# Recurrent mixer of a three-block network: both heads of a pair in one step, products of the two heads interleaved

## Chip, cores and metric

One core of a Trainium2 chip runs the whole program. The metric is the time of one execution on the device in microseconds, and the number that counts is the median of several executions. Engines are named as in the profile: TensorE (PE; its weight loads PEld), VectorE (DVE), ScalarE (ACT), GpSimd (POOL), SyncE (SP).

## What is computed

Three blocks follow each other on one sequence of 512 tokens with 1024 channels. The change lies in the mixer of the first block, which computes two things from one projection: a recurrence over 8 heads of 64 channels (RWKV-7), and attention over a window of 128 tokens with 8 query heads. The reference, cut to that:

```python
p = h @ w_in                       # 512 x 1024 times 1024 x (1792 + 768)
# recurrent heads: state is 64 x 64 per head, w_t decay, kk_t and b_t from k and a
def step(state, inp):
    r_t, w_t, k_t, v_t, kk_t, b_t = inp
    sa = einsum('bhvk,bhk->bhv', state, -kk_t)
    state = (state * w_t[:, :, None, :] + sa[..., None] * b_t[:, :, None, :]
             + v_t[..., None] * k_t[:, :, None, :])
    return state, einsum('bhvk,bhk->bhv', state, r_t)
_, o = lax.scan(step, s0, ...)     # then a norm over each head, a bonus term, a gate
# attention: scores of a block of 128 queries with its own and the previous 128 keys
scores = einsum('bnqhgd,bnkhd->bnhgqk', qb, kb) * (HEAD_DIM ** -0.5)
probs = softmax(concatenate([masked scores, sink]))[..., :-1]
out = einsum('bnhgqk,bnkhd->bnqhgd', probs, vb)
x = x + concatenate([o_rwkv, o_attn]) @ w_out
```

## The kernel before

The kernel keeps channels on the 128 partitions and the 512 tokens along the free side. A **dense** product is a tile of 128 channels in and 128 out on 512 tokens; for precision it is done three times, with weights and activations split into a high and a low part (L390, L391, L392, on the two banks ps_d). A projection of 128 output channels is 24 of them. In the trace each dense product is one record, and each product of plain fp32 operands is two records.

The mixer of the first block (class Mixer1, function mixer_1) cuts the recurrence into 8 chunks of 64 tokens, so that it becomes products of 64x64 blocks. A **pair** i (0 to 3) is two heads, h = 0 and 1, whose 64 channels lie on the lower and the upper half of the partitions. Eight chunks are numbered c, or (j, e) with c = 2j + e. Five generators are stepped in turn by rounds, in the order of the letters of a string, here 'DZADHPHA':

- D, project: the 20 projections in the order of a list, three dense products a step, and at the end the output projection (mixed).
- P, per_token and pre: what each token of a pair needs, then its turned copies (L841 turns v, L854 and L863 turn k and b).
- H, heads and head: the chunk-local work of a pair. heads steps the two heads of a pair in turn.
- Z, all_states, states and finish: what links the chunks.
- A, attention and attend: four steps c of two query heads, four blocks j of 128 queries each.

The scheduler turns the steps into one instruction stream for each engine; each engine takes its stream in order. What one generator waits for is thus covered by what the others have put behind it in TensorE's stream.

The function head, for one head: two sets of four products of 64 rows and 128 columns (L918, tile pa, half e each), read by VectorE into X, kk and rb (L921 to L924); eight products pk (L928), read into ak and a4 (L930, L931); eight products pv (L938), copied by ScalarE into R; then a triangular inverse: two steps of px (L952) with X = 1 - px (L953), and for each of four levels l the products pw (L966, read into W, L969) and px (L973, taken off X), with VectorE's turning of X into T between. Each is a chain: product, VectorE, product. Eight products write both halves of a tile: the one for chunk (j, e) lies on the column half e, and its rows are on half e too, except for pk and pv. Last come four products on the whole array, pg (L988), whose results ScalarE puts into gk and gv (L997). Tiles are [128, 4, 64] and have two buffers, one for each head.

The function states, for a pair: three sets of sixteen products (L1015; 128 rows, 64 columns; eight chunks of head 0 and then eight of head 1) with a reader each; the chain of six steps through the chunks (L1032, L1033); two sets of sixteen for the output (L1042 and L1049, on the bank ps_z). finish: the gate product (L1063), its readers L1066 and L1067, the product for the variance (L1069), the norm and the result in bv. The last pair's result is split in two (k and r, L404 and L405) and read by the last products of the stage (L1191 to L1193, in the function last).

attend: scores of two heads (L1121: 64 rows, 128 columns, up to 256 streamed), each with its own bank of ps_p and its own step, softmax, turning of the weights on TensorE (L1145), and the output (L1152; 128 rows, 64 columns, head 0 on the column half 0, head 1 on the half 1).

The eight banks: ps_d 2, ps_m 3 (all of head, the sets of states, finish), ps_p 2, ps_z 1.

## Time and profile before

| what | value |
|---|---|
| median of the runs | 2809.36 us (2806.97, 2809.36, 2810.24) |
| the profiled execution | 2807.89 us; its span, from first to last instruction, 2806.0 us |
| TensorE busy | 2762.4 us, 98% of the span |
| VectorE, ScalarE, GpSimd busy | 60%, 41%, 3% |
| the stage from L841 at 412.73 to the end of L1049 at 722.69 | 309.96 us |

All times of the trace are from the start of that span. The span is 1.9 us shorter than the time of its execution, and this execution is 1.5 us below the median. A row of the timeline gives the start, the time until the last of its records ends, the engine, the line, the operation with out<-in, for a product the size of the part of the array that it uses (rows * columns) and the streamed operand, and the number of records. Products are pipelined: rows overlap, and the distance between two starts says what a product costs, not its length.

### The profile page before, as it was taken

What the parts mean: (1) busy time and instruction counts of PE and PEld (TensorE: products, weight loads), DVE (VectorE), ACT (ScalarE), POOL (GpSimd) and SP (SyncE); (2) the same over time, 40 slices, a digit from 0 to 9 for tenths busy, and PEclk for the clock granted to TensorE, in tenths of its full rate; (3) what the DMA queues carried; (4) which work ended last, traced back from release to release, by engine and by line L of the source; (5) the groups of instructions that cost most, each with busy time, mean ns of one, the idle gap of its engine ahead of it and who ended that gap; (6) DMA issues with size and microseconds to landing.
All of it is one profiled execution on the core that took longest, in us unless ns stands there. A gap on an engine that the chain in (4) does not pass through costs nothing. (4 is left out here: it accounts for less than half of the span.)

```text
span 2806.0 us, 36273 instructions
## 1 busy us (share of the span) xinstructions
PE 2762.4 (98%) x14502; PEld 2245.7 (80%) x14502; DVE 1682.7 (60%) x2795; ACT 1161.1 (41%) x1779; POOL 79.8 (3%) x167
## 2 busy tenths in 40 slices
PE   8999999999999999999999999999999999999998
PEld 7888877777788888777888888888887878888887
DVE  5443466777643436687344894646845985556456
ACT  4222354454332224575333433444457544343333
POOL 0000000000000000000000011110000000000000
PEclk9999999999999999999999999999999999999999
DMA  4333231101233333322343354443224443322232
GB/s 139 98 98 98 87 127 44 31 31 56 67 98 98 98 97 125 121 76 81 96 132 98 106 165 140 139 133 109 86 71 144 144 150 106 114 74 83 68 105 76
DMA packets 83866, 281.19 MB, mean 100 GB/s; under 512 B 10096, under 2 KB 10608, under 8 KB 82928
## 3 DMA queue, kind: packets, MB, share of 16 engines
q1 hardware_dynamic: 76464, 255.28, 28.3%
q0 software_dynamic: 5888, 18.09, 1.8%
q10 hardware_dynamic: 1344, 5.49, 0.5%
q8 instruction: 114, 1.87, 0.3%
q14 instruction: 56, 0.46, 0.1%
HBM read 254.44 MB, written 23.07 MB: 99 GB/s over the span
## 5 line engine op out<-in xcount | busy, mean ns | idle before, releaser
L366 ACT CAST whi<-raw 128x1024 fp32r<-128x1024 f32 (+4 forms) x454 | 450.6, 993 | 1204.3 <-PE ps_d L391 817.1
L390 PE MATMUL ps_d<-xhi,whi 128*128 128x512 f32 x1896 | 753.9, 398 | 12.7 <-ACT whi L366 8.1
L392 PE MATMUL ps_d<-xhi,wlo 128*128 128x512 f32 x1896 | 742.3, 392 | 3.4 <-DVE wlo L367 3.4
L391 PE MATMUL ps_d<-xlo,whi 128*128 128x512 f32 x1896 | 742.6, 392 | 0.2 <-DVE xlo L458 0.2
L367 DVE TENSOR_TENSOR wlo<-raw,whi 128x1024 fp32r<-128x1024 f32 (+4 forms) x454 | 521.4, 1149 | 156.3 <-ACT whi L366 155.0
L390 PEld LDWEIGHTS ps_d<-xhi,whi 128*128 128x128 f32 x1896 | 356.9, 188 | 93.1 <-ACT whi L366 8.6
L392 PEld LDWEIGHTS ps_d<-xhi,wlo 128*128 128x128 f32 x1896 | 357.0, 188 | 80.0 <-DVE wlo L367 4.9
L391 PEld LDWEIGHTS ps_d<-xlo,whi 128*128 128x128 f32 x1896 | 357.3, 188 | 75.5 <-issue 4.0
L390 PE MATMUL ps_d<-hh,whi 128*128 128x512 f32 x608 | 237.2, 391 | 0.4 <-ACT hh L404 0.4
L391 PE MATMUL ps_d<-hl,whi 128*128 128x512 f32 x608 | 237.0, 390 | 0.2 <-DVE hl L405 0.2
L392 PE MATMUL ps_d<-hh,wlo 128*128 128x512 f32 x608 | 236.7, 389 | 0.3 <-DVE wlo L367 0.3
L390 PEld LDWEIGHTS ps_d<-hh,whi 128*128 128x128 f32 x608 | 114.1, 188 | 25.1 <-ACT hh L404 0.9
L391 PEld LDWEIGHTS ps_d<-hl,whi 128*128 128x128 f32 x608 | 114.1, 188 | 24.5 <-DVE hl L405 1.1
L392 PEld LDWEIGHTS ps_d<-hh,wlo 128*128 128x128 f32 x608 | 114.1, 188 | 24.3 <-DVE wlo L367 0.7
L625 DVE TENSOR_TENSOR hb<-ps_d,rstd 128x512 f32<-128x512 f32 x44 | 30.4, 691 | 136.1 <-PE ps_d L392 136.1
L632 DVE SCALAR_TENSOR_TENSOR x<-ps_d,x 128x512 f32<-128x512 f32 x48 | 33.2, 692 | 116.2 <-PE ps_d L392 116.2
L390 PE MATMUL ps_d<-mixhi,whi 128*128 128x512 f32 x224 | 89.0, 397 | 0.8 <-DVE x L1674 0.7
L392 PE MATMUL ps_d<-mixhi,wlo 128*128 128x512 f32 x224 | 88.0, 393 | 0.0
L624 DVE TENSOR_TENSOR ha<-ps_d,rstd 128x512 f32<-128x512 f32 x44 | 30.4, 691 | 95.8 <-PE ps_d L392 93.2
L391 PE MATMUL ps_d<-mixlo,whi 128*128 128x512 f32 x224 | 87.6, 391 | 0.0
L469 DVE TENSOR_TENSOR acc<-acc,sq 128x512 f32<-128x512 f32 x67 | 46.0, 687 | 25.7 <-ACT sq L468 25.1
L1473 DVE TENSOR_TENSOR x<-ps_d,x 128x512 f32<-128x512 f32 x32 | 22.0, 688 | 61.3 <-PE ps_d L392 61.3
(692 smaller groups left out, 4151.2 us busy)
## 6 DMA issues: line engine op xcount, KB each, us to landing
raw<-in_ffn_gu_dram SPq DMA_DIRECT2D x88, 512.0 KB, 3.5
raw<-in_w_in_dram SPq DMA_DIRECT2D x64, 512.0 KB, 3.5
raw<-in_ffn_dn_dram SPq DMA_DIRECT2D x32, 512.0 KB, 3.5
raw<-in_w_up_dram SPq DMA_DIRECT2D x32, 512.0 KB, 3.5
raw<-in_w_down_dram SPq DMA_DIRECT2D x32, 512.0 KB, 3.9
raw<-in_ret_in_dram SPq DMA_DIRECT2D x32, 512.0 KB, 3.2
raw<-in_ab_in_dram SPq DMA_DIRECT2D x28, 512.0 KB, 3.2
raw<-in_ret_v_dram SPq DMA_DIRECT2D x16, 512.0 KB, 3.2
```

Source lines behind the costliest of these rows:

```text
L366: nc.scalar.copy(hi[:, :n], raw[:, :n])
L367: nc.vector.tensor_sub(lo[:, :n], raw[:, :n], hi[:, :n].bitcast(F32))
L390: PE.matmul(ps, lhsT=hi[:, w], rhs=ah, start=first, stop=False)
L391: PE.matmul(ps, lhsT=hi[:, w], rhs=al, start=False, stop=False)
L392: PE.matmul(ps, lhsT=lo[:, w], rhs=ah, start=False, stop=last)
L469: nc.vector.tensor_add(acc, acc, sq)
L624: nc.vector.tensor_mul(a, pg, r)
L625: nc.vector.tensor_mul(b, pu, r)
L632: nc.vector.scalar_tensor_tensor(out=xm, in0=po, scalar=0.5, in1=xm, op0=ALU.mult, op1=ALU.add)
L1473: nc.vector.tensor_add(xm, po, xm)
```

## The change

Both heads of a pair become one generator, head_pair, and one chain. Where head made eight products in a step, head_pair makes sixteen, and VectorE's and ScalarE's operations read both heads at once, on tiles [128, 8, 64] with one buffer. The results go to a new tile ps_h of two banks; ps_m keeps one bank, for the sets of states and for finish. The string of turns loses one H. Within a step the two heads alternate: in pa, pg and the sets of sixteen h is the innermost loop, and in the sets of eight a list gives the halves e = 0, 1, 1, 0 and so on, head 0 and head 1 in turn. In attend both scores are issued before the first mask is added, and the output's loop over heads becomes the inner one. finish waits until the projection l1 is done. Lines move by 3 to 7: L918 becomes L921, L928 L931, L938 L941, L952 L957, L966 L972, L973 L978, L988 L994, L1015 L1021, L1032 L1038, L1042 L1047, L1049 L1054, L1063 L1069, L1069 L1075, L1121 L1127, L1145 L1152 and L1152 L1159.

```diff
     def heads(self):
         for i in range(4):
             yield from self.until(lambda: self.qs[i] is not None)
-            pair = [self.head(i, h, self.qs[i]) for h in range(2)]
-            while pair:
-                for g in list(pair):
-                    if next(g, pair) is pair:
-                        pair.remove(g)
-                    yield
+            yield from self.head_pair(i, self.qs[i])
             self.qs[i]["ready"] = True
...
+    def ph(self):
+
+        return self.m.ps.tile([P, 2, S], F32, tag="h", name="ps_h", bufs=self.m.nb["h"])
...
-        tile = lambda tag: self.t(tag, 2, (P, 4, 64))
-        each = [(j, e, HALF[e]) for j in range(4) for e in range(2)]
...
+        tile = lambda tag: self.t(tag, 1, (P, 8, 64))
+
+        each = [(h, j, (e + h) % 2) for j in range(4) for e in range(2) for h in range(2)]
+        each = [(4 * h + j, j, e, HALF[e], HALF[h]) for h, j, e in each]
...
-            pa = four(self.pm())
+            pa = eight(self.ph())
             for j in range(4):
-                mm(pa[:, j], lhsT=q["bk"][hs, j, 2 * e:2 * e + 2].rearrange("p s t -> p (s t)"),
-                   rhs=q["kr"][hs, j, :, 64 * e:64 * e + 64], start=True, stop=True)
+                for h in range(2):
+                    hs = HALF[h]
+                    mm(pa[:, 4 * h + j], lhsT=q["bk"][hs, j, 2 * e:2 * e + 2].rearrange("p s t -> p (s t)"),
+                       rhs=q["kr"][hs, j, :, 64 * e:64 * e + 64], start=True, stop=True)
...
-            px = half(self.pm())
-            for j, e, he in each:
-                mm(px[he, j], lhsT=a4[he, j], rhs=X[he, j], start=True, stop=True)
+            px = half(self.ph())
+            for g, j, e, he, hs in each:
+                mm(px[he, g], lhsT=a4[he, g], rhs=X[he, g], start=True, stop=True)
...
         for n in range(3):
             ps = eight(self.pm())
-            for h in range(2):
-                hs = HALF[h]
-                gk, rb = q["gk%d" % h], q["rb%d" % h]
-                for c in range(8):
+            for c in range(8):
+                for h in range(2):
+                    hs = HALF[h]
+                    gk, rb = q["gk"][:, 8 * h:8 * h + 8], q["rb"][:, 8 * h:8 * h + 8]
                     l, r = ((bkT[:, c, hs], gv[:, c, hs]), (gk[:, c], bkT[:, c, hs]), (gk[:, c], rb[:, c]))[n]
                     mm(ps[hs, c], lhsT=l, rhs=r, start=True, stop=True)
...
         yield
-        for h in range(2):
-            hs = HALF[h]
-            for c in range(8):
+        for c in range(8):
+            for h in range(2):
+                hs = HALF[h]
                 cs = slice(c * 64, c * 64 + 64)
                 mm(po[hs, cs], lhsT=z[hs, c], rhs=cf[hs, cs], start=False, stop=(c == 7), skip_group_check=True)
...
         nc.scalar.copy(o, po)
         yield
+        yield from self.wait("l1")
         pg = self.pm()
...
+            pss = [self.pp()[:, 0:nk] for h in range(2)]
             for h in range(2):
-                ps = self.pp()[:, 0:nk]
-                mm(ps, lhsT=self.q[HALF[h], c, js], rhs=self.k[HALF[h], k0:k0 + nk], start=True, stop=True)
-                nc.vector.tensor_tensor(out=s[:, h], in0=ps, in1=mask, op=ALU.add)
-                yield
+                mm(pss[h], lhsT=self.q[HALF[h], c, js], rhs=self.k[HALF[h], k0:k0 + nk], start=True, stop=True)
+            for h in range(2):
+                nc.vector.tensor_tensor(out=s[:, h], in0=pss[h], in1=mask, op=ALU.add)
+            yield
...
-            for h in range(2):
-                for b in range(nb):
+            for b in range(nb):
+                for h in range(2):
                     mm(po[HALF[h]], lhsT=self.vT[:, k0 // P + b, HALF[h]], rhs=pT[:, h, b],
...
-        es.enter_context(self.banks(**dict(d=2, m=3, p=2, z=1)))
+        es.enter_context(self.banks(**dict(d=2, h=1, m=1, p=2, z=1)))
...
-                   'DZADHPHA')
+                   'DZADHPA')
```

**TensorE's order in the first pair, from pk to the first steps of the inverse** (ps_m<-x is pk, a_... is a4; xhi, xlo, whi and wlo are the parts of dense operands). Before:

```order
L928 MATMUL ps_m<-x 64x64 x8
L938 MATMUL ps_m<-vs,akk 64x64 x8
L952 MATMUL ps_m<-X,a_2879 64x64 x8
L390 MATMUL ps_d<-xhi,whi 128x512
L391 MATMUL ps_d<-xlo,whi 128x512
L392 MATMUL ps_d<-xhi,wlo 128x512
L390 MATMUL ps_d<-xhi,whi 128x512
L391 MATMUL ps_d<-xlo,whi 128x512
L392 MATMUL ps_d<-xhi,wlo 128x512
L938 MATMUL ps_m<-vs,akk 64x64 x8
L952 MATMUL ps_m<-X,a_2899 64x64 x8
L952 MATMUL ps_m<-X,a_2879 64x64 x8
```

After (L941 is pv, L957 is px; L392 ends one group of dense products, L1097 turns v for attention):

```order
L941 MATMUL ps_h<-vs,akk 64x64 x16
L392 MATMUL ps_d<-xhi,wlo 128x512
L1097 MATMUL ps_p<-cst,z 128x128 x4
L957 MATMUL ps_h<-X,a_2878 64x64 x16
L390 MATMUL ps_d<-xhi,whi 128x512
L391 MATMUL ps_d<-xlo,whi 128x512
L392 MATMUL ps_d<-xhi,wlo 128x512
L390 MATMUL ps_d<-xhi,whi 128x512
L957 MATMUL ps_h<-X,a_2878 64x64 x16
```

Two visits of eight became one of sixteen, and between two steps of one chain the other head's products no longer stand; dense products do.

**TensorE's order in the fourth pair, the same steps** (L1032 is the chain of states of the third pair, amix the operand of the output projection, L863 turned copies of this pair). Before:

```order
L928 MATMUL ps_m<-x 64x64 x3
L938 MATMUL ps_m<-vs,akk 64x64
L863 MATMUL ps_p<-cst,x 128x128 x4
L938 MATMUL ps_m<-vs,akk 64x64 x7
L391 MATMUL ps_d<-amix,whi 128x512
L952 MATMUL ps_m<-X,a_5514 64x64 x8
L1032 MATMUL ps_z<-z,ms 64x64 x2
L938 MATMUL ps_m<-vs,akk 64x64 x8
L952 MATMUL ps_m<-X,a_5544 64x64 x8
L952 MATMUL ps_m<-X,a_5514 64x64 x8
L1032 MATMUL ps_z<-z,ms 64x64 x2
L952 MATMUL ps_m<-X,a_5544 64x64 x8
```

After (L1038 is the chain of states, L1152 turns softmax weights, L1159 makes attention outputs):

```order
L931 MATMUL ps_h<-x 64x64 x4
L863 MATMUL ps_p<-cst,x 128x128 x4
L931 MATMUL ps_h<-x 64x64 x12
L1038 MATMUL ps_z<-z,ms 64x64 x2
L941 MATMUL ps_h<-vs,akk 64x64 x16
L1038 MATMUL ps_z<-z,ms 64x64 x4
L957 MATMUL ps_h<-X,a_5374 64x64 x8
L1152 MATMUL ps_p<-cst,sc 128x128 x4
L957 MATMUL ps_h<-X,a_5374 64x64 x8
L1038 MATMUL ps_z<-z,ms 64x64 x2
L1159 MATMUL ps_p<-pT,avT 64x128 x4
L957 MATMUL ps_h<-X,a_5374 64x64 x16
```

Before, the eight products of the other head stand between two steps of one head; after, two to four products of L1038, L1152 and L1159 do, and between the last two steps of L957 nothing but L1038 and L1159.

**VectorE's order in the fourth pair** (L930 and L931 read pk of one head, L1122 to L1131 are the softmax, L1033 the chain of states). Before:

```order
L930 TENSOR_TENSOR ak<-ps_m,m_2450 128x256
L1122 TENSOR_TENSOR sc<-ps_p,m_2450 128x256
L931 TENSOR_TENSOR a_5514<-ps_m,m_2450 128x256
L1125 TENSOR_REDUCE anm<-sc 128x2
L932 TENSOR_TENSOR X<-X,m_2450 128x256
L1126 TENSOR_SCALAR anm<-anm 128x2
L1033 SCALAR_TENSOR_TENSOR z<-ps_z,pcs,ns 128x64
L1127 TENSOR_TENSOR anm<-anm,vec 128x2
L930 TENSOR_TENSOR ak<-ps_m,m_2450 128x256
L1129 TENSOR_TENSOR aes<-vec,anm 128x2
L931 TENSOR_TENSOR a_5544<-ps_m,m_2450 128x256
```

After (L933 and L934 read pk of both heads):

```order
L1129 TENSOR_TENSOR sc<-ps_p,m_2450 128x256 x2
L935 TENSOR_TENSOR X<-X,m_2450 128x512
L1132 TENSOR_REDUCE anm<-sc 128x2
L933 TENSOR_TENSOR ak<-ps_h,m_2450 128x512
L1133 TENSOR_SCALAR anm<-anm 128x2
L934 TENSOR_TENSOR a_5374<-ps_h,m_2450 128x512
L1134 TENSOR_TENSOR anm<-anm,vec 128x2
L1039 SCALAR_TENSOR_TENSOR z<-ps_z,pcs,ns 128x64
L1136 TENSOR_TENSOR aes<-vec,anm 128x2
```

One operation of 512 elements stands where two of 256 stood, with the softmax between them as before.

**TensorE's order in the tail, the last pair's finish** (k, r, sgp, a, L and e_... hold the parts of the recurrent results of pairs 0 to 2). Before, from the gate product:

```order
L1063 MATMUL ps_m<-wsg,lora 128x512
L1069 MATMUL ps_m<-cf,cst 128x512
L390 MATMUL ps_d<-k,whi 128x512
L391 MATMUL ps_d<-r,whi 128x512
L392 MATMUL ps_d<-k,wlo 128x512
L390 MATMUL ps_d<-sgp,whi 128x512
L391 MATMUL ps_d<-a,whi 128x512
L392 MATMUL ps_d<-sgp,wlo 128x512
L390 MATMUL ps_d<-L,whi 128x512
L391 MATMUL ps_d<-e_5769,whi 128x512
```

After:

```order
L1069 MATMUL ps_m<-wsg,lora 128x512
L390 MATMUL ps_d<-k,whi 128x512
L391 MATMUL ps_d<-r,whi 128x512
L392 MATMUL ps_d<-k,wlo 128x512
L390 MATMUL ps_d<-sgp,whi 128x512
L391 MATMUL ps_d<-a,whi 128x512
L392 MATMUL ps_d<-sgp,wlo 128x512
L390 MATMUL ps_d<-L,whi 128x512
L391 MATMUL ps_d<-e_5557,whi 128x512
L1075 MATMUL ps_m<-cf,cst 128x512
L392 MATMUL ps_d<-L,wlo 128x512
```

The variance product, L1069 before and L1075 after, stood right behind the gate product and now stands behind eight dense products; both use ps_m, which has one bank now.

## Rows read from the trace of the kernel before

**Rows 1.** Part 1 of the page: busy us, share of the span, instructions.

```profile
PE 2762.4 (98%) x14502; PEld 2245.7 (80%) x14502; DVE 1682.7 (60%) x2795; ACT 1161.1 (41%) x1779; POOL 79.8 (3%) x167
```

**Rows 2.** Windows: start:end, length, busy us of each engine, clock, DMA.

```profile
core 0: us, PE busy (x) PEld busy (x) DVE busy (x) ACT busy (x) POOL busy (x), PEclk, DMA share, GB/s
412.73:722.69 309.96, 307.89 (x3267) 226.80 (x3265) 216.18 (x565) 142.61 (x300) 1.65 (x13) 1.00 0.13 42
```

**Rows 3.** TensorE's waits in that stage: us in total, times, longest us.

```profile
PE ps_m L1015 <- ACT gv L997: 0.9, 2, 0.6
```

**Rows 4.** Timeline, TensorE: start us, us, operation, records; [idle].

```profile
444.52 0.40 PE L392 MATMUL ps_d<-xhi,wlo 128*128 128x512 f32 x1
444.85 0.66 PE L973 MATMUL ps_m<-W,T 64*64 64x32 f32 x16
445.43 0.50 PE L390 MATMUL ps_d<-xhi,whi 128*128 128x512 f32 x1
445.77 0.39 PE L391 MATMUL ps_d<-xlo,whi 128*128 128x512 f32 x1
446.00 0.40 PE L392 MATMUL ps_d<-xhi,wlo 128*128 128x512 f32 x1
```

**Rows 5.** Timeline, TensorE: one set of sixteen of L1015.

```profile
472.87 1.90 PE L1015 MATMUL ps_m<-bkT,gk 128*64 128x64 f32 x32
474.70 0.50 PE L390 MATMUL ps_d<-xhi,whi 128*128 128x512 f32 x1
```

**Rows 6.** Timeline, TensorE: four products of one head, and two on different halves.

```profile
414.93 1.16 PE L918 MATMUL ps_m<-x 64*128 64x128 f32 x8
...
392.44 0.69 PE L770 MATMUL ps_p<-wsg,lora 64*128 64x512 f32 x1
392.45 0.69 PE L775 MATMUL ps_p<-wsg,lora 64*128 64x512 f32 x1
```

**Rows 7.** TensorE's groups: records | busy us, mean ns | idle.

```profile
L918 PE MATMUL ps_m<-x 64*128 64x128 f32 x128 | 18.4, 286 | 0.0
...
L1015 PE MATMUL ps_m<-rb,gk 128*64 128x64 f32 x128 | 7.8, 225 | 0.0
```

**Rows 8.** Timeline, TensorE: attention output, and a visit on the whole array.

```profile
463.27 0.66 PE L1152 MATMUL ps_p<-pT,avT 128*64 128x128 f32 x8
...
467.66 1.05 PE L988 MATMUL ps_m<-R,xb 128*128 128x128 f32 x8
```

**Rows 9.** Timeline, TensorE: the scores of two heads.

```profile
481.19 1.14 PE L1121 MATMUL ps_p<-akey,aq 64*128 64x256 f32 x4
```

**Rows 10.** Timeline, fourth pair: a step of VectorE and the product behind it.

```profile
664.10 0.42 DVE L953 SCALAR_TENSOR_TENSOR X<-ps_m,m 128x256 f32<-128x256 f32 x1
...
664.67 0.68 PE L952 MATMUL ps_m<-X,a 64*64 64x64 f32 x16 [0.49 <-DVE asm L1137]
```

**Rows 11.** VectorE's and ScalarE's groups, same columns.

```profile
L367 DVE TENSOR_TENSOR wlo<-raw,whi 128x1024 fp32r<-128x1024 f32 x14 | 17.0, 1219 | 0.3 <-ACT whi L366 0.2
...
L864 ACT COPY bkT<-ps_p 128x512 f32<-128x512 f32 x8 | 4.6, 584 | 3.4 <-PE ps_p L863 3.3
...
L1017 DVE TENSOR_TENSOR ns<-ps_m,pcs 128x512 f32<-128x512 f32 x4 | 2.8, 692 | 4.5 <-PE ps_m L1015 4.5
```

**Rows 12.** Timeline of the tail: gate, variance and last products.

```profile
724.39 1.02 PE L1063 MATMUL ps_m<-wsg,lora 128*128 128x512 f32 x2
...
725.24 1.02 PE L1069 MATMUL ps_m<-cf,cst 128*128 128x512 f32 x2
...
725.45 0.75 DVE L1066 SCALAR_TENSOR_TENSOR bv<-bv,vec,ps_m 128x512 f32<-128x512 f32 x1 [5.86 <-PE ps_m L1063]
...
726.11 0.74 DVE L1067 SCALAR_TENSOR_TENSOR ns<-z,vec,ps_m 128x512 f32<-128x512 f32 x1
...
737.32 0.69 DVE L405 TENSOR_TENSOR r<-bv,k 128x512 fp32r<-128x512 f32 x1 [0.90 <-ACT k L404]
...
738.33 0.40 PE L1193 MATMUL ps_d<-r,whi 128*128 128x512 f32 x1
```

More of the change, by code (lines that the diff above doesn't have):

```diff
@@ L984, in head @@
         yield from self.until(lambda: i == 0 or self.step[i - 1] >= 2)
[L986 removed]
+        pg = eight(self.ph())
         for j in range(4):
[L988 to L993 removed]
+            for h in range(2):
+                mm(pg[:, 4 * h + j], lhsT=xb[:, 4 * h + j], rhs=R[:, 4 * h + j], start=True, stop=True)
+        q["gv"] = self.t("gv", 1, (P, 8, P))
+        for e in range(2):
+            ho = HALF[1 - e]
+            nc.scalar.copy(q["gv"][ho, e::2], q["vs"][ho])
         for e in range(2):
```

87 lines of the change are left out of this document (41 added, 46 removed).

## The prediction

> **What bounds the kernel now.** The page's first part [rows 1] gives TensorE 2762.4 of 2806.0 us, 98%, VectorE 60%, ScalarE 41%. I then cut out the stage that the change touches, by windows: from the first turning of v (L841, 412.73) to the last output product of the recurrent heads (L1049, 722.69) [rows 2]. There TensorE is busy for 307.89 of 309.96 us at granted clock 1.00 (the 2.4 GHz level), and TensorE's list of waits for other engines has three entries, the largest of 0.9 us [rows 3]: the stage lasts as long as TensorE needs to issue its products. So the timeline is read for the distance from one product to the next, not for busy time. An fp32 product leaves two records there (four products are "x8"), a dense one leaves one.
>
> Five distances carry the sum. (a) Dense products follow each other every 0.23 us [rows 4]. (b) A visit of eight 64x64 products between dense ones (L973): 444.52 to 445.77 is 1.25 us where two dense steps would have been 0.46, so the visit costs 0.79 [rows 4]. Its 16 records take (0.66 - 0.22)/15 = 0.029 us each: neighbours on opposite halves (e = 0, 1) run in pairs, 0.058 a pair. Streaming is 8 x 0.058 = 0.47, and the remaining 0.32 is the price of two changes of shape, 0.16 each. (c) Sixteen products of which eight in a row lie on one half (L1015, first h = 0, then h = 1): 472.87 to the next dense product at 474.70 is 1.83 us, (1.90 - 0.22)/31 = 0.054 a record, so little is paired but a few at the seam [rows 5]. For the eight of L973 that distance is 0.58 [rows 4]. (d) Four 64x128 products of one head (L918): (1.16 - 0.29)/7 = 0.124 a record [rows 6]. (e) Two products on different row halves with 128 columns do pair when they are neighbours: L770 and L775 start at 392.44 and 392.45 [rows 6]. What is taken off the length of a row, 0.22 or 0.29, is the last record's own time, by the means of L1015 and L918 [rows 7].
>
> **The change part by part.**
>
> *Sets of sixteen.* L1015 (three kinds of product, 128 records each, so 12 sets of 32 records [rows 7]), L1042 and L1049 (one set of sixteen a pair of heads in the code, 4 each) are the serial case (c). With h inside c, neighbours stand on opposite halves. The nearest row for a paired stream is (b): 0.58 + 8 more products x 0.058 = 1.05 instead of 1.83. Saving 0.78 x 20 = 15.6 us. Bounds: nothing for the sets with 128 rows if column halves cannot pair, and the full 15.6. I take the full one, because L1152 is of that form (128 rows, 64 columns): its 8 records take (0.66 - 0.29)/7 = 0.053 each, where L988 with as many streamed columns on the whole array takes (1.05 - 0.29)/7 = 0.109 [rows 8].
>
> The Trainium skill speaks against these sets: "TensorE: Matmul & The Clock Gate", Part 3, The mechanism, says a weight load overlaps running products only when the row group differs; by it the 16 sets with 128 rows would keep their 1.83 us and the time would be 2798 us instead of 2786. The L1152 row disagrees with it.
>
> *First products of a head* (L918, L921 after): 64 products, 128 records [rows 7], now alternating row halves. By (e) each four lose half of their stream, 4 x 2 x 0.11 / 2 = 0.44 us (0.109, L988's rate for as many columns [rows 8], since 0.124 holds the entry too); 16 fours: 7.0 us. Lower bound 0, since (e) is one pair in the trace.
>
> *Steps of the two heads in one visit.* The 64x64 steps (L928, L938, L952, L966, L973) are paired already, so their streams stay the same; two visits of 8 become one of 16. Along TensorE's order from L841 to the last of L1049 (L1054) the shape changes 297 times before and 255 times after; 42 x 0.16 = 6.7 us. The new row of halves is 0, 1, 1, 0: half of the neighbours now share a half, but each half still gets the same number, and the engine would only have to take the second of a pair before or with the first. Bounds: no loss, or one lost pairing at each of the 305 such neighbours (seven in each of 44 visits, three of them split in the order; L931's rows alternate), 305 x 0.058 = 17.7 us; I take no loss, because L1152 stands as h0 h0 h1 h1 before and is paired all the same [rows 8].
>
> *Attention.* The two scores stand side by side in 11 of 16 places (5 before), but the second mostly waits for ScalarE to empty a bank of ps_p: two side by side take 1.14 us in the row, more than half a microsecond each, so they did not pair [rows 9]. I take 0.9 us, within 0 to 4. L1152's new order: nothing, it is paired already.
>
> *VectorE and ScalarE.* 24 operations a head become about 24 a pair: 256 elements cost 0.42 [rows 10], 512 cost 0.69 [rows 11], so a pair saves 0.15 each, some 14 of 216 us. VectorE is at 70% [rows 2] and would be at 202/280 = 72%. This hides wholly behind TensorE, but a single step gets longer, and that is the next term.
>
> *New waits.* Each step needs the last product's own 0.22, then 0.04 until VectorE starts (L1063 ends at 725.41, L1066 starts at 725.45 [rows 12]), its operation, and 0.15 to the next product (L953 ends at 664.52, L952 goes on at 664.67 [rows 10]). For 512 elements that is 1.10 us, for 256 it is 0.83. Where dense products stand between, n of them cover 0.15 + 0.34 + 0.23 (n - 1) + 0.33 [rows 4]: 1.5 us for four, 2.0 for six. In the first three pairs the order puts 4 to 20 there, so the waits are covered. In the fourth pair dense work is used up. There I add, place by place: pv (L941) behind pk, whose one bank is read by ak and a4 (0.22 + 0.04 + 2 x 0.69 + 0.15 = 1.79) and covered by two L1038 (3 x 0.058): 1.6 us; the first px behind ScalarE's copy of pv (0.58 [rows 11] + 0.41, against four L1038 at 5 x 0.058): 0.7; the turning of the softmax (L1152 after) queued on VectorE behind W: 1.5; three places where a set of L1021 follows its predecessor in the single bank of ps_m (1.10 against 0.80): 0.9; pg behind the two subtractions of xb and the dense product after it: 1.2; the second half of pa behind three readers: 0.4; five smaller ones: 1.5. Sum 7.8. The stage of before has some 1.4 of its own in those places (0.49 at 664.67 [rows 10], 0.9 at L1015 [rows 3]) that go. Net 6.4, bounds 0 and 20: a wait whose cover I counted can still be queued behind a 1.22 us operation of VectorE [rows 11].
>
> *The tail.* With one bank for ps_m, the variance product (L1069; L1075 after) can no longer follow the gate product at once: it waits for both readers of the gate's bank, L1066 and L1067, which end at 726.85, and so starts at about 727.0 instead of 725.24, 1.8 later [rows 12]. Its chain ends in L405 at 738.01, and L1193, which needs that, stands at 738.33 [rows 12]: 0.15 of the 1.8 is slack, the dense work left is the same, nothing covers the rest. Cost 1.6 us, bounds 0 and 3.
>
> *Sum.* 15.6 + 7.0 + 6.7 + 0.9 = 30.2 saved, 6.4 + 1.6 = 8.0 given back, 22.2 net. The weight transfers must keep up with a stage 7% shorter: DMA is at 13% there [rows 2]. The profiled execution took 2807.89 us (span 2806.0), 1.5 under the median 2809.36 and within the three runs. 2807.9 - 22.2 = 2785.7, **2786 us**.
>
> **Rivals.**
> 1. *The waits are covered better than counted*: 2807.9 - 30.2 + 1 = 2779 us. For it: stalls add cover to one another.
> 2. *VectorE's queue delays covered steps too* (20 instead of 6.4): 2799 us. For it: 72% load and single operations of 1.22 us; against: 4 to 20 dense products between steps.
> 3. *Column halves do not pair* (16 sets x 0.78 = 12.5 lost): 2798 us. Against it stands L1152's row alone. The Trainium skill's sentence on weight loads, cited above, is this mechanism.
> 4. *The 0, 1, 1, 0 row breaks the pairs* (17.7 lost): 2804 us, no change that can be told.
> 5. *Slower: the chain of one pair sets the pace.* Before, one head's products stood between two steps of the other; now only other work does. A step left bare costs 1.10 - 0.06 = 1.0 us. There are 60 steps; the saving (30.2 - 1.6 = 28.6) is gone when 29 of them are bare, and with 45 bare the time is 2824 us. Against: the order leaves about ten bare.
> 6. *The change does not do what it says*: the engine already pairs over the seam as in L1152, so the sets gain less than half (8 us fewer), 2794 us. Against it the 1.83 us of (c).
>
> **How the numbers follow.** Chances: forecast 0.54, rival 1 0.13, rival 2 0.13, rival 3 0.04, rival 4 0.05, rival 5 0.06, rival 6 0.05. The forecast's own spread is 2781 to 2792. Leaving out rivals 4 and 5 and the lower edge of rival 1 gives 2774 to 2801. A measurement can tell 0.2% (5.6 us) from no change. Below 2803.7: forecast and rivals 1, 2, 3, 6, 0.89; within: rival 4 and the near end of rival 5, 0.06; slower: 0.05.
>
> **What would show it.** After: a set of L1021 with 1.05 us to the next dense product and not 1.83; L921 near 0.06 a record; L972 and L978 as x32 with 0.029 a record (0.04 or more would be rival 4); TensorE's waits for VectorE or ScalarE near 8 us and nearly all in the fourth pair (in every pair: rival 2 or 5); L1075 about 1.8 us later behind L1054 than before. The stage, 309.96 us, at about 290. The forecast is wrong if the pairs do not form, or if bare steps appear in pairs one to three.

## The result

The changed kernel takes 2795.1 us in the median (2792.8 to 2796.7, four runs), the kernel before 2809.8 us beside it. The ratio is 0.9946 with a 95% interval of 0.9929 to 0.9963: 15 us faster, where 22 were forecast. The profiled execution took 2792.8 us, its span is 2790.8 us, 15.2 us less than before.

Two views answer to [rows 1] and [rows 2], with the same columns; first part 1 of the page:

```profile
PE 2737.6 (98%) x14502; PEld 2224.3 (80%) x14502; DVE 1674.2 (60%) x2699; ACT 1156.4 (41%) x1758; POOL 79.5 (3%) x165
```

Then the window from the first record of L841 to the end of the last of L1054:

```profile
413.09:706.79 293.70, 283.36 (x3269) 206.59 (x3267) 208.35 (x469) 137.91 (x279) 1.62 (x13) 0.98 0.13 43
```

The window of [rows 2] ends 0.27 us before the last record of L1049 does; to the end of that record the stage took 310.2 us before. It takes 293.7 now, 16.5 less. Two things in this row are new. TensorE is busy for 283.4 of 293.7 us, so it now idles 10 us in the stage and not 2. And its granted clock is 0.98 where it was 1.00.

A step of two heads (L978, answers to [rows 4]), a set of sixteen (L1021, answers to [rows 5]) and eight first products (L921, answers to [rows 6]) on the timeline:

```profile
437.68 1.12 PE L978 MATMUL ps_h<-W,T 64*64 64x32 f32 x32
...
480.06 1.15 PE L1021 MATMUL ps_m<-bkT,gk 128*64 128x64 f32 x32
481.14 0.50 PE L390 MATMUL ps_d<-xhi,whi 128*128 128x512 f32 x1
...
496.10 1.16 PE L921 MATMUL ps_h<-x 64*128 64x128 f32 x16
497.11 1.02 PE L775 MATMUL ps_p<-wsg,lora 64*128 64x512 f32 x2
```

One more kind of step, which the prediction passed over: eight products pk before, sixteen now.

```profile
422.63 0.68 PE L928 MATMUL ps_m<-x 64*64 64x64 f32 x16
...
500.93 0.69 PE L931 MATMUL ps_h<-x 64*64 64x64 f32 x32
```

The set costs 1.08 us to the next dense product; it was 1.83. The sixteen products of L978 take (1.12 - 0.22)/31 = 0.029 us a record, as the eight of L973 did. The eight first products make a row of 1.16 us (1.01 us to the next start), as long as that of four before. And the sixteen products pk take no longer than eight did: (0.69 - 0.22)/31 = 0.015 us a record, where L928 has (0.68 - 0.22)/15 = 0.031.

TensorE's waits for other engines in the stage (us in total, times, longest), which answer to [rows 3]:

```profile
PE ps_h L972 <- DVE X L980: 1.9, 1, 1.9
PE ps_h L941 <- DVE anm L1134: 1.6, 1, 1.6
PE ps_p L1152 <- DVE sc L1148: 1.3, 2, 0.9
PE ps_h L931 <- DVE rb L927: 1.3, 2, 1.0
PE ps_d L390 <- ACT whi L366: 0.9, 1, 0.9
PE ps_d L390 <- ACT L L404: 0.9, 1, 0.9
PE ps_p L1159 <- ACT pT L1154: 0.8, 2, 0.5
PE ps_d L390 <- ACT amix L404: 0.5, 1, 0.5
PE ps_z L1038 <- DVE z L1039: 0.5, 1, 0.5
```

They add up to 9.7 us; before there were three, 1.9 together. By their place on the timeline only 3.7 us of them lie in the fourth pair (from 634 us on), where the prediction had put all of its 7.8; another 3.7 lie at the end of the third (617 to 625 us) and the rest earlier. The longest lies in the third pair, which the prediction had called covered. Its place on the timeline:

```profile
617.31 1.02 PE L829 MATMUL ps_p<-s,cst 128*128 128x512 f32 x2
...
617.80 0.68 DVE L810 TENSOR_TENSOR a<-kk,a 128x512 f32<-128x512 f32 x1
...
618.39 0.68 DVE L820 TENSOR_TENSOR x<-kk,sgp 128x512 f32<-128x512 f32 x1
...
619.07 0.68 DVE L826 TENSOR_TENSOR x<-a,L 128x512 f32<-128x512 f32 x1
...
619.67 0.15 DVE L1134 TENSOR_TENSOR anm<-anm,vec 128x2 f32<-128x2 f32 x1
619.74 0.41 DVE L980 TENSOR_TENSOR X<-X,ps_h 128x256 f32<-128x256 f32 x1
...
620.21 1.12 PE L972 MATMUL ps_h<-X,ak 64*64 64x32 f32 x32 [1.88 <-DVE X L980]
```

VectorE works without a gap through the per-token work of the fourth pair (L810, L820, L826) and the softmax (L1134 and two more); L980, for which the one chain of the third pair waits, stands behind them all. What follows is seen in windows of 10 us:

```profile
613.00:623.00 10.00, 7.52 (x100) 5.29 (x96) 9.86 (x25) 5.94 (x14) 0.28 (x1) 0.99 0.54 203
623.00:633.00 10.00, 8.67 (x41) 6.37 (x39) 7.70 (x20) 3.12 (x10) 0.00 (x0) 0.67 0.08 23
633.00:643.00 10.00, 9.85 (x139) 7.47 (x139) 6.26 (x14) 2.96 (x9) 0.00 (x0) 1.00 0.09 34
...
653.00:663.00 10.00, 9.01 (x206) 8.05 (x208) 5.41 (x17) 4.58 (x11) 0.00 (x0) 0.83 0.01 3
```

VectorE is busy for 9.86 of the first 10 us, TensorE for 7.52. The mean clock is then 0.67, and 0.83 after the next wait (L941, at 652 us). With levels of 2.4 and 1.2 GHz a mean of 0.67 is 6.6 of 10 us at the lower one, 0.83 is 3.4: some 10 us in all, and at most 5 us lost by it. No row of before has such a stretch in this stage, and the prediction has no term for it. Over the whole span the granted clock is 0.994 or 0.995 in the four executions of the changed kernel; in twenty of before (beside e9 to e11) it is 0.995 to 0.998, and they take from 2804.5 us (at 0.998) to 2814.4 us (at 0.995). So much of the scatter of before goes with its clock.

### The profile page after: what moved, and what is told of

Its sections match the earlier page's. It is cut to its first block, busy times and chain, and to the rows that moved or that the text cites. A ratio compares the mean times of both kernels' runs of the same rounds, so it can differ in the third digit from the quotient of the medians.

```text
span 2790.8 us, 36154 instructions
## 1 busy us (share of the span) xinstructions
PE 2737.6 (98%) x14502; PEld 2224.3 (80%) x14502; DVE 1674.2 (60%) x2699; ACT 1156.4 (41%) x1758; POOL 79.5 (3%) x165
## 5 line engine op out<-in xcount | busy, mean ns | idle before, releaser
L366 ACT CAST whi<-raw 128x1024 fp32r<-128x1024 f32 (+4 forms) x454 | 450.5, 993 | 1207.8 <-PE ps_d L391 809.9
L390 PE MATMUL ps_d<-xhi,whi 128*128 128x512 f32 x1896 | 752.2, 397 | 13.9 <-ACT whi L366 9.3
L392 PE MATMUL ps_d<-xhi,wlo 128*128 128x512 f32 x1896 | 743.0, 392 | 3.5 <-DVE wlo L367 3.4
L367 DVE TENSOR_TENSOR wlo<-raw,whi 128x1024 fp32r<-128x1024 f32 (+4 forms) x454 | 521.2, 1148 | 156.1 <-ACT whi L366 154.6
L392 PEld LDWEIGHTS ps_d<-xhi,wlo 128*128 128x128 f32 x1896 | 356.9, 188 | 80.9 <-DVE wlo L367 5.3
L392 PE MATMUL ps_d<-hh,wlo 128*128 128x512 f32 x608 | 236.8, 390 | 0.5 <-DVE wlo L367 0.5
L392 PEld LDWEIGHTS ps_d<-hh,wlo 128*128 128x128 f32 x608 | 114.1, 188 | 24.9 <-DVE wlo L367 1.4
L392 PE MATMUL ps_d<-mixhi,wlo 128*128 128x512 f32 x224 | 87.7, 392 | 0.0
```

The source lines that it names most:

```text
L366: nc.scalar.copy(hi[:, :n], raw[:, :n])
L367: nc.vector.tensor_sub(lo[:, :n], raw[:, :n], hi[:, :n].bitcast(F32))
L390: PE.matmul(ps, lhsT=hi[:, w], rhs=ah, start=first, stop=False)
L392: PE.matmul(ps, lhsT=lo[:, w], rhs=ah, start=False, stop=last)
```

## Experiments

The stage below is always the window from the first record of L841 to the end of the last output product of the heads (L1054; L1049 in kernels made from before), with TensorE's mean granted clock in it. It is read from one profile each, and no second profile of a kernel shows how far it scatters; ratios are to the kernel before beside it. A change of shape is a place in the stage where the part of the array that TensorE uses (rows * columns) differs from one record to the next; where the prediction counted 297 and 255 in the order, the records have 298 and 256.

| kernel | stage us | clock in it | changes of shape | median us | ratio (95% interval) |
|---|---|---|---|---|---|
| before | 310.2 | 1.00 | 298 | 2809.8 | 1 |
| changed | 293.7 | 0.98 | 256 | 2795.1 | 0.9946 (0.9929 to 0.9963) |
| e1 sets in the old order | 307.6 | 0.98 | 251 | 2808.0 | 0.9993 (0.9984 to 1.0002) |
| e2 halves 0, 1, 0, 1 | 297.2 | 0.98 | 268 | 2795.9 | 0.9944 (0.9926 to 0.9962) |
| e3 one wait filled | 292.3 | 0.99 | 256 | 2792.9 | 0.9939 (0.9924 to 0.9954) |
| e4 pv in ps_m | 295.4 | 0.98 | 262 | 2797.9 | 0.9948 (0.9928 to 0.9968) |
| e5 before, sets alone | 300.3 | 1.00 | 322 | 2798.2 | 0.9970 (0.9956 to 0.9983) |
| e6 fourth pair split | 313.2 | 0.95 | 283 | 2810.9 | 1.0009 (0.9999 to 1.0018) |
| e7 two waits filled | 292.3 | 0.99 | 256 | 2791.4 | 0.9939 (0.9922 to 0.9955) |
| e8 before, sets and scores | 305.6 | 0.98 | 316 | 2804.3 | 0.9984 (0.9974 to 0.9993) |
| e9 split, one wait filled | 313.0 | 0.95 | 283 | 2810.9 | 1.0007 (0.9997 to 1.0016) |
| e10 norm on GpSimd | 298.9 | 0.97 | 258 | 2798.6 | 0.9959 (0.9944 to 0.9973) |
| e11 turns DZADPHA | 305.8 | 0.96 | 292 | 2806.2 | 0.9987 (0.9977 to 0.9996) |
| e12 first products in the old order | 298.2 | 0.97 | 256 | 2798.5 | 0.9955 (0.9938 to 0.9972) |

### e1: the sets in the old order

```diff
-            for c in range(8):
-                for h in range(2):
+            for h in range(2):
+                for c in range(8):
```

in the three places of states. 

> The changed kernel with the products of the sets of sixteen (L1021, L1047, L1054) put back in the old order, eight of head 0 and then eight of head 1; all else as changed. Theory A (the sums of the prediction hold product by product, 0.78 us a set, and the shortfall comes from waits and from the clock): the stage from L841 to the end of L1054, 293.7 us in the changed kernel, gets 13 to 16 us longer, 307 to 310 us, and the kernel is back at 2807 to 2811 us. Theory B (the sets pair only in part, and this is where the missing gain went): 6 to 10 us longer, 2801 to 2805 us. If column halves could not pair at all, only the four sets of L1054 would count, 3 us.

The stage got 13.9 us longer, 307.6 us, and the kernel is back at 2808.0 us, not to be told from before. That is theory A. The sets with 128 rows pair too: four sets of L1054 alone would have been 3 us. And it says more than was asked: without the sets, all the rest of the change is worth 2.6 us of the stage and nothing that can be measured in the whole. Added up from each start to the next start on TensorE, the sets alone take 24.2 us in the changed kernel, 37.8 in e1 and 37.3 before.

### e12: the first products in the old order

```diff
-            for j in range(4):
-                for h in range(2):
+            for h in range(2):
+                for j in range(4):
```

in pa alone. 

> The changed kernel with the first products of a pair (L921) in the old order, four of head 0 and then four of head 1; the order on TensorE is otherwise the same, row for row. Theory A (neighbours on different row halves pair, as L770 and L775 do): in the changed kernel L921 shows 0.073 us a record inside its visits against 0.121 for L918 before, 128 records, so the stage gets 5 to 7 us longer, 299 to 301 us, if none of it falls into a wait. Theory B (these products stand in front of VectorE's reads, so that what is saved on TensorE is waited for, or 64x128 products do not pair): less than 2 us longer.

The stage got 4.5 us longer. A visit of eight on the timeline of e12, which stands beside the 1.01 us above:

```profile
497.13 1.71 PE L921 MATMUL ps_h<-x 64*128 64x128 f32 x16
498.68 1.02 PE L775 MATMUL ps_p<-wsg,lora 64*128 64x512 f32 x2
```

1.55 us instead of 1.01. Added up over the 128 records, from each start to the next start on TensorE, L921 takes 15.04 us here and 11.47 in the changed kernel: 3.6 of the 4.5 us are its own. The rest was not taken apart; the clock is lower, 0.51 in the stretch from 623 to 633 us where the changed kernel has 0.67. The products pair, but the whole is below theory A's 5 to 7 us: the term of 7.0 us was too large.

### e2: the halves in the row 0, 1, 0, 1

```diff
-        each = [(h, j, (e + h) % 2) for j in range(4) for e in range(2) for h in range(2)]
+        each = [(h, j, e) for j in range(4) for h in range(2) for e in range(2)]
```

> The changed kernel with the list of a step in the order of halves 0, 1, 0, 1 instead of 0, 1, 1, 0 (both chunks of head 0, then both of head 1). Theory A: two neighbours on one half cost nothing as long as each half gets the same number; L972 and L978 stay near 0.029 us a record and the stage within 2 us of 293.7. Theory B (the row 0, 1, 1, 0 loses pairings): these steps get faster, to less than 0.028 a record, and the stage by 3 us or more.

Visits of L972 and L978, one of each from the timeline of e2:

```profile
445.32 1.12 PE L972 MATMUL ps_h<-X,ak 64*64 64x32 f32 x32
...
447.97 1.12 PE L978 MATMUL ps_h<-W,T 64*64 64x32 f32 x32
```

They take 1.12 us as in the changed kernel: two neighbours on one half cost nothing. The stage is 3.5 us longer all the same, outside the 2 us that theory A gave it, with waits of nearly the same sum, 12 more changes of shape (1.9 us at 0.16 each) and a longer time at the lower clock (means of 0.75, 0.91, 0.79 and 0.87 from 623 to 643 and 653 to 673 us). The median is that of the changed kernel. So the row of halves is settled: in both rows the first and second product, the third and fourth and so on lie on opposite halves. What made the stage longer is the order that the scheduler gave to the rest, and the clock, which is not the same here although the two long waits (L972 and L941) are.

### e5 and e8: parts of the change on the kernel before

e5 changes only the loops of the sets in the kernel before, here the first of the three:

```diff
-            for h in range(2):
-                hs = HALF[h]
-                gk, rb = q["gk%d" % h], q["rb%d" % h]
-                for c in range(8):
+            for c in range(8):
+                for h in range(2):
+                    hs = HALF[h]
+                    gk, rb = q["gk%d" % h], q["rb%d" % h]
```

> The kernel before with one part of the change alone: the products of the sets of sixteen (L1015, L1042, L1049) with the heads alternating; two chains of heads, three banks of ps_m and all else as before. The sets put back in the changed kernel made its stage 14.0 us longer and left 2.6 us of the whole gain, so theory A' says that the two heads in one step give back nearly all that they save (first products 5, changes of shape 7, against waits 8 and the clock 3), and this kernel is as fast as the whole change: a stage of 295 to 298 us, 2794 to 2798 us. Theory B' says that the gains do not add and the sets need the wide steps: at most 8 us, 2802 us or more.

e8 has besides this the scores side by side:

```diff
+            pss = [self.pp()[:, 0:nk] for h in range(2)]
             for h in range(2):
-                ps = self.pp()[:, 0:nk]
-                mm(ps, lhsT=self.q[HALF[h], c, js], rhs=self.k[HALF[h], k0:k0 + nk], start=True, stop=True)
-                nc.vector.tensor_tensor(out=s[:, h], in0=ps, in1=mask, op=ALU.add)
-                yield
+                mm(pss[h], lhsT=self.q[HALF[h], c, js], rhs=self.k[HALF[h], k0:k0 + nk], start=True, stop=True)
+            for h in range(2):
+                nc.vector.tensor_tensor(out=s[:, h], in0=pss[h], in1=mask, op=ALU.add)
+            yield
```

> The kernel before with two parts of the change: the sets of sixteen with the heads alternating, and the scores of two heads issued side by side (L1121). Scores as L1127 of the changed kernel took 15.8 us of TensorE's order and 17.3 us before. Theory A: 1 to 2 us less than with the sets alone, 2793 to 2796 us, below the changed kernel or the same. Theory B (a second bank of ps_p held longer delays the other users of ps_p): no gain over the sets alone, or up to 2 us longer.

e5 came out between the two theories: a stage of 300.3 us, 10.0 less than before. The set itself, from e5's timeline, is as cheap as in the changed kernel, and TensorE's list of waits in the stage has three short entries:

```profile
475.17 1.15 PE L1015 MATMUL ps_m<-bkT,gk 128*64 128x64 f32 x32
476.25 0.50 PE L390 MATMUL ps_d<-xhi,whi 128*128 128x512 f32 x1
```

```profile
PE ps_m L988 <- DVE xb L981: 1.1, 1, 1.1
PE ps_p L1152 <- ACT pT L1147: 0.3, 1, 0.3
PE ps_m L1015 <- ACT gk L996: 0.2, 1, 0.2
```

The sets themselves, from start to start, take 23.7 us, 13.6 less than before, so they do not need the wide steps. What is missing to that fits the changes of shape: the scheduler put other products in between, and there are 322 where the kernel before has 298. At 0.16 us each, 24 more are 3.8 us. So the sets alone bring six tenths of the stage's gain, and the other parts another 6.6 us on top, not nothing as theory A' had it, though in the times of the whole kernel the intervals of e5 and of the changed kernel still overlap: what each part is worth depends on the order that the scheduler makes of the others. The runs of e5 spread from 2796.0 to 2807.1 us; the profiled one took 2803.6.

e8 is worse than e5 by 5.4 us of the stage: waits of 1.8 us (L988 for xb, two) and 1.5 us (L938 for rb) stand in it and the clock fell to 0.83 and 0.66 in two stretches. The scores' own records take 15.6 us from start to start and 16.9 in e5; what the new order of the steps does outweighs that.

### e3 and e7: waits filled with work that nobody reads

e3, and in e7 both lines:

```diff
-        mm(pb, lhsT=m.const("bones"), rhs=t, start=True, stop=True)
+        for _ in range(3 if i == 3 else 1): mm(pb, lhsT=m.const("bones"), rhs=t, start=True, stop=True)
...
-            for g, j, e, he, hs in each:
+            for g, j, e, he, hs in each * (2 if (i, l) == (2, 5) else 1):
                 mm(px[he, g], lhsT=T[he, g], rhs=W[he, g], start=True, stop=True)
```

> The changed kernel with the product of the bonus term of the fourth pair (L829) issued three times into the same bank instead of once: two fp32 products more, 1.7 us of TensorE's work, in the place where TensorE waits 1.9 us for VectorE (L972 for L980, at 618 us) and behind which the granted clock is 0.67 for 10 us. Nothing else moves. Theory A (the idle time lets the clock fall, and half of the slow stretch is lost besides the wait): with the wait filled the clock stays at 1.00 or falls later and for less, and the stage gets 2 to 4 us shorter although more is computed. Theory B (the clock's fall is not tied to this wait, or costs nothing because TensorE waits there anyway): the stage stays within 0.5 us, or gets up to 1 us longer.

> The kernel with the product L829 of the fourth pair issued three times, and besides the sixteen products of L978 of the last level of the third pair issued twice, 0.9 us of work in the place where TensorE waits 0.9 us for the softmax (L1152 for L1148), in front of the 3.3 us at half clock that were left there. Theory A (idle time lets the clock fall): the clock stays at 1.00 from 612 to 640 us and the stage gets another 1 to 1.6 us shorter than the 292.25 us with L829 filled alone, though more is computed. Theory B: the clock falls all the same, and the stage stays within 0.3 us or gets up to 1 us longer.

Windows of 2 us from 618 us on, of the changed kernel first, then of e3 and, one window, of e7:

```profile
618.00:620.00 2.00, 0.33 (x1) 0.00 (x0) 2.00 (x6) 1.84 (x3) 0.00 (x0) 1.00 0.71 287
620.00:622.00 2.00, 1.68 (x37) 1.32 (x39) 1.86 (x7) 1.78 (x5) 0.00 (x0) 1.00 1.02 434
622.00:624.00 2.00, 1.13 (x33) 1.00 (x33) 2.00 (x9) 0.63 (x4) 0.00 (x0) 0.71 0.54 229
624.00:626.00 2.00, 1.54 (x7) 0.89 (x8) 1.96 (x5) 0.60 (x2) 0.00 (x0) 0.50 0.00 0
626.00:628.00 2.00, 2.00 (x7) 1.35 (x7) 1.19 (x4) 0.04 (x1) 0.00 (x0) 0.50 0.00 0
```

```profile
618.00:620.00 2.00, 2.00 (x5) 0.57 (x3) 2.00 (x6) 1.86 (x3) 0.00 (x0) 1.00 0.70 262
620.00:622.00 2.00, 1.73 (x38) 1.30 (x37) 1.86 (x7) 1.76 (x5) 0.00 (x0) 1.00 1.03 442
622.00:624.00 2.00, 1.10 (x33) 0.99 (x33) 2.00 (x9) 0.65 (x4) 0.00 (x0) 1.00 0.54 229
624.00:626.00 2.00, 1.54 (x9) 0.97 (x10) 1.96 (x5) 0.64 (x2) 0.00 (x0) 1.00 0.00 0
626.00:628.00 2.00, 2.00 (x10) 1.67 (x9) 1.97 (x5) 0.00 (x0) 0.00 (x0) 0.58 0.00 0
```

```profile
626.00:628.00 2.00, 2.00 (x11) 1.85 (x10) 1.97 (x6) 0.00 (x0) 0.00 (x0) 0.56 0.00 0
```

With 618 to 620 us filled the clock falls 4 us later, and the fall at 653 us is gone, although L941 waits its 1.6 us there as before. The stage got 1.4 us shorter with 1.7 us more work in it: the direction is theory A's, the size is below its 2 to 4, and the ratios of the two kernels overlap. e7 then filled the wait for the softmax; the clock still fell at 626 us and the stage stayed where it was, which is theory B's outcome for that place. So the wait of L972 takes part in the clock's fall: with it filled, two kernels out of two spend some 3 us of the stage at the lower clock, and the changed kernel 10. But filling one more wait is not enough to keep the clock up.

### e4: pv in the bank of ps_m

```diff
-        pv = half(self.ph())
+        pv = self.pm().rearrange("p (g t) -> p g t", g=8)
```

> The changed kernel with the product pv (L941) written to the bank of ps_m instead of ps_h, so that it no longer waits until VectorE has read pk from ps_h. Theory A (bank waits of the fourth pair and the clock behind them cost what they show): L941's wait of 1.6 us at 652 us goes, the clock at 653 to 663 us is 1.00 and not 0.83, and the stage gets 2 to 4 us shorter. Theory B (the chain of VectorE is the limit there and the bank only the last of several waits): the wait moves to the next step (L957 for R's or X's operands) and the stage gains less than 1 us.

The 1.6 us went, and L957 waits 0.8 us in its place; the clock is 1.00 from 653 to 663 us, and falls later (0.85 from 683 to 693 us). But the order changed along the whole stage, a wait of 1.1 us for pb (L726) came in, and the clock from 623 to 633 us is 0.58 and not 0.67. The stage is 1.7 us longer. The wait itself was as priced; taking it away gains nothing. This is nearer to theory B. The runs of e4 do not lie close together: three took 2797.4 to 2799.0 us and one 2788.9.

### e6 and e9: the fourth pair in two chains

The function takes the heads of a chain as an argument, (0, 1) for three pairs, (0,) and (1,) for the fourth; the core:

```diff
-            yield from self.head_pair(i, self.qs[i])
+            pair = [self.head_pair(i, q, hh) for hh in (((0,), (1,)) if i == 3 else ((0, 1),))]
+            while pair:
+                for g in list(pair):
+                    if next(g, pair) is pair:
+                        pair.remove(g)
+                yield
```

> The changed kernel with its fourth pair in two chains again, one for each head, stepped in one turn, each with its own bank of one ps_h tile; the first three pairs as changed. Theory A: in the fourth pair, where TensorE has no dense products left, one head's products cover the other's step; L941's wait of 1.6 us and the smaller ones there go, at the price of some 14 more changes of shape (2 us) where nothing stood between; the stage gets 1 to 3 us shorter than 293.7 and the clock's fall near 653 us is gone. Theory B (these waits come from VectorE's load, not from the single chain): the waits stay or move, and the stage gets 0 to 3 us longer.

e9 issues eight of its products five times, in the longest wait:

```diff
-            for g, j, e, he, hs in each:
+            for g, j, e, he, hs in each * (5 if (i, l, hh) == (3, 4, (0,)) else 1):
                 mm(pw[he, g], lhsT=ak[he, g], rhs=odd(X[he, g]), start=True, stop=True)
```

> The kernel with the fourth pair split in two chains (stage 313.2 us) with eight of its products (L989, head 0, level 4 of the fourth pair) issued five times instead of once, 1.9 us of work in the place where TensorE waits 1.7 us (684 to 686 us) and behind which the granted clock is 0.50 for 20 us with TensorE busy all the time. Nothing else moves. Theory A (the idle time starts the slow stretch, and the slow stretch costs about 10 us): the clock stays at 1.00 from 683 to 713 us and the stage is 8 to 10 us shorter, 303 to 305 us. Theory B (the clock falls there for what TensorE does afterwards, many short products and few dense ones, not for the wait): it falls all the same and the stage is 0 to 2 us longer.

Neither theory on e6 held: the stage is 19.5 us longer, and the kernel as slow as before. Its waits are not much longer than the changed kernel's (11 us by the list). The difference is here, first e6 and then e9:

```profile
684.00:686.00 2.00, 0.49 (x16) 0.38 (x14) 2.00 (x6) 0.00 (x0) 0.00 (x0) 0.74 0.00 0
686.00:688.00 2.00, 1.37 (x22) 1.24 (x24) 1.43 (x4) 0.62 (x1) 0.15 (x1) 0.50 0.00 0
688.00:704.00 16.00, 16.00 (x117) 11.39 (x114) 6.71 (x15) 2.96 (x6) 0.00 (x0) 0.50 0.19 58
704.00:706.00 2.00, 2.00 (x12) 1.86 (x11) 0.00 (x0) 0.07 (x1) 0.00 (x0) 0.64 0.00 0
```

```profile
684.00:686.00 2.00, 1.64 (x56) 1.65 (x58) 1.99 (x6) 0.00 (x0) 0.00 (x0) 1.00 0.00 0
686.00:688.00 2.00, 1.53 (x47) 1.31 (x44) 1.41 (x4) 0.15 (x1) 0.04 (x1) 1.00 0.00 0
688.00:690.00 2.00, 1.68 (x19) 1.43 (x20) 1.60 (x4) 1.03 (x3) 0.11 (x1) 0.69 0.03 8
690.00:704.00 14.00, 14.00 (x99) 9.75 (x98) 5.74 (x12) 2.40 (x5) 0.00 (x0) 0.50 0.22 67
704.00:706.00 2.00, 2.00 (x12) 1.86 (x11) 0.00 (x0) 0.07 (x1) 0.00 (x0) 0.64 0.00 0
```

In e6 TensorE is busy for every one of the 16 us from 688 to 704, at half clock. Added up over windows of 10 us by the reckoning above, e6 spends 34 us of the stage at the lower clock, 17 us lost at most, against 10 us and 5 in the changed kernel: up to 12 of the 19.5 us. Another 4 go with 27 more changes of shape at 0.16 us, where some 14 had been counted on. In e9 the long wait was nearly gone, TensorE was busy for 1.64 of the 2 us where it had been for 0.49, and the clock fell 4 us later and stayed low until the same place. Theory A of e9, that this one wait starts the slow stretch, fell. What TensorE does in the slow stretch (visits of eight 64x32 products between groups of three dense ones) it does from 676 to 684 us of the same kernel at a clock of 1.00. The cause of the long slow stretch stays open.

### e10 and e11: two ways to move the longest wait

```diff
-        nc.vector.tensor_mul(y, gb, y)
-        nc.vector.tensor_add(bv, bv, y)
+        late = nc.vector if i == 3 else nc.gpsimd
+        late.tensor_mul(y, gb, y)
+        late.tensor_add(bv, bv, y)
```

> The changed kernel with the last two operations of the norm of pairs 0 to 2 (L1079, L1080, 0.69 us each on VectorE) on GpSimd instead. In the third pair they stand at 613.3 and 614.5 us in VectorE's queue, which is full from 612 to 620 us and for which TensorE waits 1.9 us (L972 for L980). Theory A (VectorE's queue makes this wait, the wait starts the slow clock): the wait gets 1.2 to 1.4 us shorter, the clock's fall at 622 us smaller or gone, and the stage 1.5 to 4 us shorter, 290 to 292 us. Theory B (another step of the chain is as late, or GpSimd delays the pair's result and with it the dense products of the output): within 1 us of 293.7 or longer.

```diff
-                   'DZADHPA')
+                   'DZADPHA')
```

> The changed kernel with the turns in the order DZADPHA instead of DZADHPA, so that the per-token work is written ahead of the heads. In TensorE's order the last steps of the third pair then stand behind nine and ten dense products each instead of one to five. Theory A (the waits are a matter of where the dense products stand): the 1.9 us wait of L972 for L980 goes, and the clock's fall behind it; the other waits of the fourth pair stay; the stage is 2 to 5 us shorter, 289 to 292 us, and the kernel at 2789 to 2793 us. Theory B (dense work spent there is missing later): the sum of the waits stays, and the stage is within 2 us of 293.7.

In both the wait of L972 for L980 is gone from the list, and another stands at its head, first e10's and then e11's:

```profile
PE ps_d L390 <- DVE pb L726: 2.8, 2, 2.5
```

```profile
PE ps_d L390 <- DVE anm L1138: 2.6, 1, 2.6
```

VectorE's queue makes a dense product wait instead of a step. The stage is 5 and 12 us longer than the changed kernel's, with clocks of 0.97 and 0.96; in e11 TensorE is busy for all of 663 to 673 us at half clock. For e10 that is theory B. In e11 the waits keep their sum within 1.5 us, as theory B said, but its 2 us for the stage were far off: there are 36 more changes of shape, 5.8 us at 0.16 each, besides the clock.

No kernel here is clearly better than the changed one. e7, which only fills two waits, is the fastest at 2791.4 us, 3.7 us under it; the intervals of the two ratios overlap.

## Why the prediction was right, and where it was not

The time lies in the range of 2774 to 2801 us and on the forecast side. The gain is two thirds of what was forecast, 15 of 22 us.

- **What bounds the kernel**: right. The stage is as long as TensorE needs, and it is 16.5 us shorter, and the rest of the span gives 1.3 us of that back.
- **Sets of sixteen**, 15.6 us: e1 gives 13.9. The price of one set was right (1.08 us measured, 1.05 expected), but the first set of a pair is cut in three pairs of four: in the first pair L1021 stands in pieces of four, two and twenty-six records with dense products between, and a piece of one product pairs with nothing and pays its own changes of shape. Rival 3 is refuted for this form: 128 rows, neighbours on different column halves, and the set at 1.08 us. The sentence that the prediction cites for rival 3 from the Trainium skill ("TensorE: Matmul & The Clock Gate", Part 3, The mechanism: a weight load overlaps running products only when the row group differs) does not agree with that row.
- **First products**, 7.0 us: e12 gives 4.5, of which 3.6 are their own. Mechanism right, size wrong by half: the prediction halved a steady stream of four, but visits are short, and their entry does not shrink. In the visit shown, the first product's two records start 0.21 us apart in e12 and in the changed kernel alike; only behind them do two products share the 0.11 us between two starts that one record took before. And not all of them do: at 567 us fifteen records of L921 make a row of 1.41 us, where the sixteen shown make 1.16.
- **Fewer visits**, 6.7 us for 42 changes of shape: 42 fewer in the records too. Not undone alone; e5, with 24 more, fits the price of 0.16 us. The row of halves 0, 1, 1, 0 costs nothing, as taken (e2); rival 4 is out (its sum gives 2803.4 us, not 2804).
- **The products pk**, no term: the prediction took the 64x64 steps as paired already, with streams that stay the same. For L931 that was wrong. Its row half goes by the head and its column half by the list, so that sixteen products of both heads lie on all four quarters of the array, and a record takes 0.015 us instead of 0.031: about 2 us over its 128 records.
- **Scores**, 0.9 us: L1127 takes 15.8 us from start to start where L1121 took 17.3. On the kernel before the same edit lost 5 us of the stage (e8 against e5), by what it does to the order.
- **New waits**, 6.4 us net: 9.7 - 1.9 = 7.8. L941's 1.6 us was exact, but that the sum was near is luck: the fourth pair has 3.7 us of waits and not 7.8, and the first three, which were called covered, have the other 6. The largest one lies in the third pair, where the prediction counted 4 to 20 dense products as cover and did not see that at 616 us the projections end while VectorE has a finish, a pair's per-token work and a softmax in its queue at once. That is rival 2's mechanism at one place.
- **The tail**, 1.6 us: L1075 came 1.9 us later behind L1054 than L1069 behind L1049, as worked out, but from the end of the stage to the last product it is 23.4 us and was 23.0. The step that failed is that the chain behind it had only 0.15 us of slack. Before, splits of weights (L366 and L367, 0.93 and 1.22 us) stood inside the chain of the norm; in the changed kernel L435 and L436, and L1079 and L1080, follow each other (one L367 still stands in front of L1079). From the first operation of the norm (L1071, L1077 after) to the end of L405 the chain takes 10.4 us and took 11.7.
- **The clock**, no term: the failed step. The prediction read 1.00 in [rows 2] and took every wait at its own length. At most 5 us were lost in the two slow stretches. Filling one wait shortened both together by two thirds and brought 1.4 us, so by that rate the whole cost about 2 us.

The terms together, as far as they were measured: 13.9 + 3.6 + 6.7 (42 x 0.16) + 2.0 (pk) + 1.5 - 7.8 = 19.9 us, 3.4 more than the measured 16.5. The clock, 2 to 5 us, is of the size to take that; but the terms come from different kernels, and e1 has waits and a clock of its own, so this is a reckoning and not a proof. The prediction's gross saving was 30.2; 27.7 came.

Why did so large a change move so little? Joining two heads in one step, with the scores, saves about 14 us of TensorE's work by these terms and gives back all but 2.6 us (e1), about 8 of it in waits and the rest perhaps by the clock. That it is because each head had been the other's cover is likely but not shown: e6, which gave the fourth pair its second chain back, did not bring the waits down. Undone, the order of products inside the sets takes nearly the whole gain with it (e1); alone it brings six tenths of it (e5).

## To carry to other kernels

Where many small products use half of the array's rows or columns, put neighbours on different halves: it was worth 0.75 us for each sixteen, needed no other engine, and made up most of this gain. Where a step has both row halves and both column halves free, use all four quarters (L931, 0.015 us a record). Before two chains are joined into one with wider steps, ask what stands between its steps then, and look at the other engines' queues at the places where the dense work runs out. Price a bare wait on TensorE above its own length (e3 got 1.4 us shorter although the 1.9 us wait was filled with 1.7 us of work), and look at the granted clock in windows of a few microseconds behind it.

## What was not expected of the hardware

- Neighbours need not alternate strictly: a row of halves 0, 1, 1, 0 runs at 0.029 us a record like 0, 1, 0, 1 (e2); each couple of products in the order still has one on either half.
- Products with 128 rows and 64 columns pair across column halves in long streams: sixteen in 1.08 us instead of 1.83.
- Sixteen 64x64 products on all four quarters of the array take as long as eight on two of them (L931, 0.69 us; L928, 0.68).
- The granted clock can stay at half for 16 us in which TensorE is busy throughout (e6, 688 to 704 us), and after waits of the same place and length it falls in one kernel and not in another (653 us: 0.83 in the changed kernel, 1.00 in e3). Neither was explained by the runs.
